# The S5 stage of a two-layer decoder trunk: copies of g as own steps, a new plan of steps, later tables loaded behind a weight

## The chip, the core and the metric

The kernel runs on one core of a Trainium2 chip. A core has several engines that each work through their own list of instructions in order and wait for one another through semaphores: TensorE (PE in the profile; its weight loads are PEld) multiplies matrices into psum, VectorE (DVE), ScalarE (ACT) and GpSimd (POOL) work element by element, and SyncE (SP) issues most of the DMA transfers from a queue of its own. The metric is the time of one execution on the device in microseconds (us). Three executions of the kernel before took 980.18, 980.32 and 984.25 us; the median is 980.32.

## The reference

Two layers over a sequence of 256 tokens of width 1024, all in float32. Each layer adds half a SwiGLU, a mixer, and another half SwiGLU to the residual h. The mixer of layer 0 is S5, a diagonal state-space layer with 64 groups of 16 channels and 64 states; that of layer 1 is an attention. The change lies in the S5 mixer, which the reference writes as follows (shapes cut):

```python
u = hn @ w_in                                   # 256 x 1024, hn = RMSNorm(h)
lam = exp((a_re + i a_im) * dt);  bb = coef * b # tables of each group
st[t] = lam * st[t-1] + bb @ u[t]               # complex states, a scan over the 256 tokens
y = re(c @ st) + d_skip * u
g = gelu(y)
g = g * sigmoid(g @ w_glu)
h = h + g @ w_out
```

## The kernel before, in words

The kernel is one long program in six phases: f00 (first SwiGLU), s5, f01, f10, moba, f11. The order of the instructions on each engine is the order in which the Python code emits them (`manual_schedule`). Products in float32 are made of three faster products: every operand is split into a high part, which the fast matmul takes exactly, and a low part (the rest). So a weight unit is loaded into one of three `raw` buffers (1 MB each), then split by halves: ScalarE writes `whi` (line 86, or line 92 where a gain is folded in) and VectorE writes `wlo` (line 87 or 93). `Stream.pump()` emits the next half's split when a slot is free, and when both halves of a unit are split its `raw` buffer is given to the next unit's load on SP's queue. In `plan` strings a pump is the word `P`.

In the phase f00 small pieces of work are dropped between the matmuls by a time plan (`tables`): they compute the tables of S5 (discretised matrices and powers of lambda) and write them to DRAM (`dA`, `dE`, `dB`). When that is done, the function loads them back for blocks b = 0, 1, 2 (lines 957 to 961): TA (512 KB), TE (260 KB), TB (768 KB), with three buffers of each. Later blocks are loaded from within the steps.

In `s5` the 1024 channels are eight blocks b of 128. Its steps, all written out in order in the string `plan`, are:

- `wC.t:k` (w_in): part k of eight of the product with w_in, for columns from C (0, 256, 512; 512 takes 512 columns) and token half t. Three matmuls (lines 399 to 401). After part 7 ScalarE copies the product from psum to `us` (line 1015) and VectorE transposes it into `U` (line 1016). These products live in the two `pM` psum tiles.
- `tb` (t1): 32 small matmul instructions with table TA (line 1025), into `pA` tiles for b below 4 and `pM` tiles above.
- `rb` (rot): ScalarE clears a column and writes `rh` (lines 1036, 1037); VectorE rotates and scans (lines 1044 to 1049); GpSimd rotates back into `hr` (lines 1051 to 1054). TE is the table.
- `yb` (y_out): 48 matmul instructions with TB on U and hr (line 1068) into a `pR` psum tile; gelu on ScalarE (`yg`, line 1072), a transpose on VectorE (`gs`, line 1074).
- `gb` (g_tr): TensorE transposes gs into a `pR` tile (line 1083). For b of 2 and above ScalarE reads the tile into g's high part (line 1086), VectorE into its low part (line 1087). In every case ScalarE then reads it a third time, into `gf` (line 1088), g in full precision. There are two `pR` tiles, shared by y and g steps.
- `ub:o` (glu): output o of eight of g @ w_glu for block b. Blocks 0 and 1 multiply gf with the raw weight in float32 (line 1106); the others use parts (lines 1108 to 1110).

Behind the plan the code issues, in loops, the last two blocks (b = 6, 7) of `glu` by pairs of outputs, each pair followed by `gate(i)` (sigmoid, times gf, split into parts: lines 1119 to 1124), and then the first two blocks of the product with w_out (`so`) with pumps between. `boundary` ends the phase.

Of the kernel before, what the change touches and what calls it, by code (L numbers as in the profile page):

```python
# [12 lines left out]
AF = mybir.ActivationFunctionType  # L13
# [107 lines left out]
def trunk_kernel(ctx: ExitStack, tc, x, ffn_norm, ffn_w_gate, ffn_w_up, ffn_w_down, mix_norm,  # L121
# [3 lines left out]
    nc = tc.nc  # L125
# [13 lines left out]
    def psR():  # L139
        return pp.tile([128, 512], F32, name="pR", tag="R", bufs=2)  # L140

    def psA(i):
        return pp.tile([128, 512], F32, name=f"pA{i}", tag=f"A{i}", bufs=1)
# [12 lines left out]
    where = {}  # L156
    WHOLE = 2
# [73 lines left out]
    def warm(func):  # L231

        w = sp.tile([128, 1], F32, name="warm", tag="warm", bufs=1)
        nc.scalar.activation(w, ones[:, 0:1], func)
# [33 lines left out]
    if "s5" in phases:  # L268
        rho = cp.tile([128, 32], F32, name="rho")
        tstack, lstack, xstack = ExitStack(), ExitStack(), ExitStack()  # L270
# [8 lines left out]
    st = Stream(nc, units, rp, hp)  # L279
# [20 lines left out]
    XP = [xp]  # L300
# [16 lines left out]
    def home(pool, ph):  # L317

        xa = pool.tile([128, 4224], F32R, name="xa")
        v = xa[:, XO[ph]:XO[ph] + 4096].rearrange("p (i k c) -> p i k c", i=2, c=256)  # L320
        return v[:, 0], v[:, 1]
# [298 lines left out]
    def tables(tp):  # L620

        V, P = nc.vector, nc.gpsimd

        def T(name, *shape):
            return tp.tile([128] + list(shape), F32, name=name)
# [41 lines left out]
        ps = psR()  # L667
# [26 lines left out]
        q, y, y2, e0, e1, den = (T(n, 32) for n in ("q", "y", "y2", "e0", "e1", "den"))  # L694
# [20 lines left out]
        ps = psR()  # L715
# [56 lines left out]
        u2, w2 = T("u2", 2, 32), T("w2", 2, 32)  # L772
# [29 lines left out]
        for i, a in enumerate((ltr, lti)):  # L802
            av = a.rearrange("p (b q) s -> p b q s", b=8)
            for k in range(2):
                P.tensor_copy(L[i][:, :, 0, k], av)
                for s in range(3):
                    o = L[i][:, :, 1, k, :, s]
# [131 lines left out]
        while work or later or dma:  # L939
# [4 lines left out]
            if later and later[0][0] <= now:  # L944
                f = later.pop(0)
                f[1](*f[2:])
                done[0] += 1
            while work and work[0][1] <= now and credit >= work[0][0] and done[0] >= work[0][4]:
                w, _, f, pe, _ = work.pop(0)
                f[0](*f[1:])  # L950
                credit -= w
                t = max([now + LAG] + [a[0] + PACE for a in later])
# [1 line left out]
            yield  # L954
        tstack.close()
        LP.append(lstack.enter_context(tc.tile_pool(name="load", bufs=3)))
        for b in range(3):
            ld_a(b)
            ld_e(b)
        for b in range(3):  # L960
            ld_b(b)

    LP, TA, TE, TB = [], {}, {}, {}

    def ld_a(b):
        TA[b] = LP[0].tile([128, 1024], F32, name="TA", bufs=3)
        nc.sync.dma_start(TA[b], dA[b])

    def ld_e(b):
        TE[b] = LP[0].tile([128, 2, 4, 65], F32, name="TE", bufs=3)  # L970
        nc.sync.dma_start(TE[b], dE[b // 4].rearrange("p (i q c) -> p i q c", i=2, c=65)[:, :, (b % 4) * 4:(b % 4) * 4 + 4])

    def ld_b(b):
        TB[b] = LP[0].tile([128, 1536], F32, name="TB", bufs=3)
        nc.sync.dma_start(TB[b], dB[b])


    def s5(nxt, entry):
        V, P = nc.vector, nc.gpsimd
        HALVES = (slice(0, 64), slice(64, 128))  # L980
        wstack = ExitStack()
        wp = wstack.enter_context(tc.tile_pool(name="s5", bufs=1))
        S, H, W = {}, {}, {}
        GT, GS = {}, {}
        acc = [None] * 4

        U = wp.tile([128, 32, 2, 32], F32, name="U")
        gf = [fp.tile([128, 640], F32, name="gf", tag=("ah", "al")[i // 2], bufs=2)[:, 0:512]
              .rearrange("p (f c) -> p f c", c=256) for i in range(4)]
# [87 lines left out]
        def g_tr(b):  # L1077
            if b == WHOLE:
                GT["h"], GT["l"] = home(xp, "g")
            ps = psR()  # L1080
            gs = GS.pop(b)
            for t in range(2):
                nc.tensor.transpose(ps[:, t * 128:(t + 1) * 128], gs[:, t].rearrange("p q c -> p (q c)"),
                                    ident)
            if b >= WHOLE:
                nc.scalar.activation(GT["h"][:, b, :], ps[:, 0:256], AF.Copy)
                V.tensor_tensor(GT["l"][:, b, :], ps[:, 0:256], GT["h"][:, b, :].bitcast(F32), op=OP.subtract)
            nc.scalar.activation(gf[b // 2][:, b % 2, :], ps[:, 0:256], AF.Copy)

        def glu(b, os):  # L1090

            u = where["glu", b // 2]
            g = gf[b // 2][:, b % 2, :]
            if b < WHOLE:
                w = st.raw[u][:, b % 2 * 1024:b % 2 * 1024 + 1024]
            else:
                gh, gl = GT["h"][:, b, :], GT["l"][:, b, :]
                wh, wl = st.get(u, b % 2)
            for o in os:
                first, last = b == 0 and o % 2 == 0, b == NB - 1  # L1100
                if first:
                    acc[o // 2] = psA(o // 2)
                d = acc[o // 2][:, (o % 2) * 256:(o % 2) * 256 + 256]
                c = slice(o * 128, o * 128 + 128)
                if b < WHOLE:
                    mm(d, w[:, c], g, start=first, stop=last, skip_group_check=True)  # L1106
                else:
                    mm(d, wh[:, c], gh, start=first, stop=False, skip_group_check=True)
                    mm(d, wh[:, c], gl, start=False, stop=False, skip_group_check=True)
                    mm(d, wl[:, c], gh, start=False, stop=last, skip_group_check=True)  # L1110
                if o == 7 and b >= WHOLE:
                    st.release(u, b % 2)
                elif o == 7 and b % 2:
                    st.free_raw(u)

        def gate(i):

            sg = fp.tile([128, 2, 256], F32, name="sg", tag="gr", bufs=2)
            nc.scalar.activation(sg, acc[i].rearrange("p (a c) -> p a c", a=2), AF.Sigmoid)
            g = gf[i]  # L1120
            V.tensor_tensor(g, g, sg, op=OP.mult)
            gh, gl = (GT[p][:, 2 * i:2 * i + 2, :] for p in "hl")
            nc.scalar.activation(gh, g, AF.Copy)
            V.tensor_tensor(gl, g, gh.bitcast(F32), op=OP.subtract)

        def so(b, t, n, last=False):
            u = where["so", b]
            if b == 0:
                acc[2 * t + n] = psA(2 * t + n)
            gh, gl = (GT[p][:, 2 * b:2 * b + 2, :] for p in "hl")  # L1130
            bank_mm(acc, t, n, gh, gl, u, [0, 1], b == 0, last)

        def step(word):
            name, _, ks = word.partition(":")
            ks = [int(k) for k in ks.split("-")] if ks else []
            ks = range(ks[0], ks[-1] + 1) if ks else ()
            if name[0] == "w":
                c0, t = name[1:].split(".")
                for k in ks:
                    w_in(int(c0), int(t), k)  # L1140
            elif name[0] == "u":
                glu(int(name[1]), ks)
            elif name == "x":
                if entry:
                    prep(1, 1, "s5")
            elif name == "P":
                st.pump()
            elif name in ("gelu", "sigmoid"):
                warm(AF.Gelu_apprx_tanh if name == "gelu" else AF.Sigmoid)
            else:  # L1150
                {"t": t1, "r": rot, "y": y_out, "g": g_tr}[name[0]](int(name[1]))

        plan = """
            w0.0:0-1 P x w0.0:2-5 P w0.0:6 w0.1:0 w0.0:7 w0.1:1-4 P w0.1:5-7 w256.0:0-4 w256.1:0-1 t0 w256.0:5
            w256.1:2 P w256.0:6 r0 w256.1:3 w256.0:7 P t1 w512.0:0 w256.1:4-7 w512.0:1 r1 w512.0:2-3 t2 gelu
            r2 t3 y0 w512.0:4-5 w512.1:0-1 w512.0:6 w512.1:2 r3 w512.1:3-4 w512.0:7 w512.1:5 y1 w512.1:6-7 g0
            y2 P P u0:0-1 g1 t4 u0:2-3 r4 g2 u0:4 t5 u0:5-7 r5 u1:0 t6 y3 u1:1-2 r6 u1:3-7 u2:0-2 t7 y4 g3
            u2:3-5 r7 y5 u2:6-7 u3:0-2 y6 g4 u3:3-4 g5 u3:5-7 P u4:0 P u4:1 P u4:2 g6 y7 u4:3-4 P P u4:5-7  # L1160
            u5:0-1 sigmoid g7 u5:2-5 P u5:6-7 P
        """
        for word in plan.split():
            step(word)
        wstack.close()
        lstack.close()
        XP[0] = xstack.enter_context(tc.tile_pool(name="xt2", bufs=1))
        for i in range(4):
            glu(6, (2 * i, 2 * i + 1))
            glu(7, (2 * i, 2 * i + 1))  # L1170
            gate(i)
        for b in range(2):
            for t in range(2):
                for n in range(2):
                    so(b, t, n)
                if t == 1:
                    for i in range(2):
                        st.release(where["so", b], i)
                st.pump(2 - b * t)

        boundary(nxt, [lambda t, n: so(2, t, n), lambda t, n: so(3, t, n, True)], acc, 1.0, pumps=(1, 2))
        for b in (2, 3):
            for i in range(2):
# [157 lines left out]


    tab = tables(tabp) if "s5" in phases else iter(())
    next(tab, None)
    slot = [0]
# [42 lines left out]
    v2, rn, r2 = (sp.tile([128, 2], F32, name=n, tag=n, bufs=1) for n in ("ms2", "rn2", "rr2"))  # L1388
# [29 lines left out]
    ps = psR()  # L1418
# [72 lines left out]
```

## Time and profile before

| what | value |
|---|---|
| median of three executions | 980.32 us |
| the profiled execution | 980.45 us |
| its span, first to last instruction | 978.6 us |
| TensorE busy | 968.7 us, 99% of the span |
| VectorE, ScalarE, GpSimd busy | 690.0, 556.1, 211.8 us |
| granted TensorE clock | 1.000 |
| S5 phase in the profile | about 209.7 to 301.8 us |

How to read the rows: a row of a timeline has the start in us, the duration in us, the engine, the line of the kernel, the operation, the tiles (written <- read), the shapes, the count, and in brackets how long the engine stood idle ahead of it and what it waited for. A row of the waits has who waited and for whom, then the total in us, the number of waits and the longest. A row of the windows has the stretch, its length, and then for TensorE, its weight loads, VectorE, ScalarE and GpSimd the busy time (with the number of instructions), the granted clock, the busy share of the DMA engines and the GB/s. A row of the chain of waits has the start, the duration and the piece of work. A row of the DMA issues has the count, the size and the median us from issue to landing. A matmul's duration covers its way through the array; the next one starts before it ends, so what one costs is the distance between starts. Instructions that repeat within a row are counted after an x.

### The profile page before, as it was taken

The page shows a single profiled execution, that of the slowest core. Times are in us where ns is not written, and L with a number is a line of the kernel's source. Part 1 is how long each engine was busy: PE and PEld are TensorE (multiplying, and loading weights), DVE is VectorE, ACT ScalarE, POOL GpSimd, SP SyncE. Part 2 cuts the span into 40 slices and gives each one's busy share as a digit, 9 for nine tenths or more (in the row PEclk, how much of TensorE's full clock was granted, in tenths as well). Part 3 has the DMA queues.
Part 4 walks back from the last instruction along what each step waited for, and adds up shares of the span by engine and source line. Part 5 has one row for each costly group of instructions (what it writes and reads, how often), then busy time and mean ns, then how long its engine had stood idle before and what let it go on. Part 6 is the DMA issues. An engine that isn't in the chain of part 4 may idle for free.

```text
span 978.6 us, 17165 instructions
## 1 busy us (share of the span) xinstructions
PE 968.7 (99%) x6695; PEld 864.0 (88%) x6695; DVE 690.0 (71%) x1118; ACT 556.1 (57%) x1008; POOL 211.8 (22%) x381
## 2 busy tenths in 40 slices
PE   9999999999999999999999999999999999999998
PEld 7878787888888999999999999998888899999997
DVE  5898878667767776666567766665789667766662
ACT  7655676453377565555456555554897566655550
POOL 5961889516501000000010000000441010000000
PEclk9999999999999999999999999999999999999999
DMA  8999999987646656565546656562544646656531
GB/s 286 263 306 300 286 287 292 270 318 239 228 172 208 214 184 213 173 216 172 172 129 216 218 179 207 173 215 92 173 155 147 199 140 214 222 176 212 172 130 43
DMA packets 145505, 200.92 MB, mean 205 GB/s; under 512 B 20152, under 2 KB 117520, under 8 KB 145168
## 3 DMA queue, kind: packets, MB, share of 16 engines
q1 hardware_dynamic: 138032, 188.51, 59.4%
q0 software_dynamic: 6816, 10.71, 4.1%
q8 instruction: 52, 0.85, 0.4%
q10 hardware_dynamic: 576, 0.61, 0.3%
q14 instruction: 29, 0.24, 0.1%
HBM read 183.89 MB, written 15.76 MB: 204 GB/s over the span
## 4 chain that ended last, share of the span: by engine, by line
PE 88%; DVE 4%; POOL 2%; DMA 2%; ACT 2%; issue 1%; SPq 0%; ACTq 0%; POOLq 0%
PE pM L554 13%; PE pM L553 13%; PE pM L555 13%; PE pA L399 9%; PE pA L401 9%; PE pA L400 9%; PE pM L399 6%; PE pM L400 5%; PE pM L401 5%; DVE wlo L87 2%; DMA raw<-in_s_w_in_dram 1%; PE pR L1068 1%; POOL sc L686 1%; PE pA L1106 1%; PE pR L333 1%
## 5 line engine op out<-in xcount | busy, mean ns | idle before, releaser
L553 PE MATMUL pM<-xa,whi 128*128 128x256 f32 x1056 | 295.7, 280 | 0.0
L554 PE MATMUL pM<-xa,whi 128*128 128x256 f32 x1056 | 294.9, 279 | 0.0
L555 PE MATMUL pM<-xa,wlo 128*128 128x256 f32 x1056 | 294.6, 279 | 0.0
L93 DVE SCALAR_TENSOR_TENSOR wlo<-raw,gT,whi 128x512 fp32r<-128x512 f32 x328 | 228.1, 747 | 72.0 <-ACT whi L92 71.8
L92 ACT ACTIVATE whi<-raw,gT 128x512 fp32r<-128x512 f32 x328 | 213.8, 711 | 19.9 <-PE pA L401 15.5
L87 DVE TENSOR_TENSOR wlo<-raw,whi 128x1024 fp32r<-128x1024 f32 (+1 forms) x155 | 188.5, 1230 | 48.9 <-ACT whi L86 47.7
L554 PEld LDWEIGHTS pM<-xa,whi 128*128 128x128 f32 x1056 | 198.5, 188 | 2.6
L553 PEld LDWEIGHTS pM<-xa,whi 128*128 128x128 f32 x1056 | 198.5, 188 | 2.3
L555 PEld LDWEIGHTS pM<-xa,wlo 128*128 128x128 f32 x1056 | 198.5, 188 | 0.0
L86 ACT ACTIVATE whi<-raw 128x1024 fp32r<-128x1024 f32 (+1 forms) x155 | 159.3, 1050 | 29.5 <-DMA raw<-in_ffn_w_up_dram 11.0
L399 PE MATMUL pA<-whi,ah 128*128 128x512 f32 x352 | 138.6, 394 | 0.0
L401 PE MATMUL pA<-whi,al 128*128 128x512 f32 x352 | 137.6, 391 | 0.0
L400 PE MATMUL pA<-wlo,ah 128*128 128x512 f32 x352 | 137.6, 391 | 0.0
L399 PE MATMUL pM<-whi,xa 128*128 128x512 f32 (+1 forms) x304 | 121.8, 401 | 1.3 <-ACT us L1015 1.3
L568 ACT ACTIVATE sg<-gr 128x256 f32<-128x256 f32 x66 | 27.6, 418 | 165.7 <-DVE gr L565 165.7
L400 PE MATMUL pM<-wlo,xa 128*128 128x512 f32 (+1 forms) x304 | 115.8, 381 | 0.1
L401 PE MATMUL pM<-whi,xa 128*128 128x512 f32 (+1 forms) x304 | 115.4, 380 | 0.0
L348 POOL TENSOR_TENSOR ms<-ss 128x1 f32<-128x1 f32 x10 | 1.9, 194 | 473.2 <-ACT sq L345 473.2
L401 PEld LDWEIGHTS pA<-whi,al 128*128 128x128 f32 x352 | 66.1, 188 | 14.3
L399 PEld LDWEIGHTS pA<-whi,ah 128*128 128x128 f32 x352 | 66.1, 188 | 11.6
L400 PEld LDWEIGHTS pA<-wlo,ah 128*128 128x128 f32 x352 | 66.2, 188 | 11.4
L565 DVE TENSOR_TENSOR gr<-pM,rrow 128x512 f32<-128x512 f32 x66 | 45.5, 689 | 40.8 <-PE pM L555 40.7
(271 smaller groups left out, 1234.4 us busy)
## 6 DMA issues: line engine op xcount, KB each, us to landing
raw<-in_ffn_w_down_dram SPq DMA_DIRECT2D x44, 1024.0 KB, 5.4
raw<-in_ffn_w_gate_dram SPq DMA_DIRECT2D x80, 512.0 KB, 4.1
raw<-in_ffn_w_up_dram SPq DMA_DIRECT2D x80, 512.0 KB, 5.2
raw<-in_moba_w_qkv_dram SPq DMA_DIRECT2D x12, 1024.0 KB, 5.2
TB<-dB SPq DMA_DIRECT2D x8, 768.0 KB, 6.6
raw<-in_ffn_w_gate_dram SPq DMA_DIRECT2D x16, 256.0 KB, 4.3
raw<-in_ffn_w_up_dram SPq DMA_DIRECT2D x16, 256.0 KB, 4.7
dA<-blank SPq DMA_DIRECT2D x8, 512.0 KB, 9.9
```

What stands on the lines that cost most here:

```text
L86: nc.scalar.activation(hi[:, c], r[:, c], AF.Copy)
L87: nc.vector.tensor_tensor(lo[:, c], r[:, c], hi[:, c].bitcast(F32), op=OP.subtract)
L92: nc.scalar.activation(hi[:, c], r[:, c], AF.Identity, scale=g)
L93: nc.vector.scalar_tensor_tensor(lo[:, c], r[:, c], g, hi[:, c].bitcast(F32), op0=OP.mult, op1=OP.subtract)
L399: mm(o, xh, wh, start=start, stop=False)
L400: mm(o, xh, wl, start=False, stop=False)
L401: mm(o, xl, wh, start=False, stop=stop)
L553: mm(o, a, xh, start=k == 0 and i == 0, stop=False, skip_group_check=True)
L554: mm(o, a, xl, start=False, stop=False, skip_group_check=True)
L555: mm(o, b, xh, start=False, stop=k == 7, skip_group_check=True)
L565: V.tensor_tensor(gr, ps.rearrange("p (i c) -> p i c", i=2), Rr["row"][:, None, :].to_broadcast([128, 2, 256]), op=OP.mult)
L568: nc.scalar.activation(sg, gr[:, 0, :], AF.Silu)
```

## The change

Four things change, all in the S5 phase.

1. The third read of the psum tile in `g_tr`, the copy into `gf`, becomes a step of its own, `fb` (function `g_f`). For blocks 0 and 1 it is still emitted at once; for blocks 2 to 7 it stands where the plan says. The psum tile is kept until then (`GP`).
2. `tables` loads back TA and TE of blocks 0 and 1 only. TA and TE of block 2 and TB of blocks 0 to 2 are loaded at the start of `s5`. On SP's queue the fourth unit of w_in and the first unit of w_glu, which followed these loads, now precede them.
3. The loops behind the plan become steps (`a` for a gate, `o` for a part of the w_out product), so that pumps can stand between them.
4. The plan is laid out anew: same steps, another order, `P` in other places.

```diff
@@ tables
         LP.append(lstack.enter_context(tc.tile_pool(name="load", bufs=3)))
-        for b in range(3):
+        for b in range(2):
             ld_a(b)
             ld_e(b)
-        for b in range(3):
-            ld_b(b)
@@ s5, g_tr
             if b >= WHOLE:
                 nc.scalar.activation(GT["h"][:, b, :], ps[:, 0:256], AF.Copy)
                 V.tensor_tensor(GT["l"][:, b, :], ps[:, 0:256], GT["h"][:, b, :].bitcast(F32), op=OP.subtract)
-            nc.scalar.activation(gf[b // 2][:, b % 2, :], ps[:, 0:256], AF.Copy)
+            GP[b] = ps
+            if b < WHOLE:
+                g_f(b)
+
+        def g_f(b):
+            if b in GP:
+                nc.scalar.activation(gf[b // 2][:, b % 2, :], GP.pop(b)[:, 0:256], AF.Copy)
@@ s5, step
+            elif name[0] == "a":
+                if name == "a0":
+                    wstack.close()
+                    lstack.close()
+                    XP[0] = xstack.enter_context(tc.tile_pool(name="xt2", bufs=1))
+                gate(int(name[1]))
+            elif name[0] == "o":
+                b = int(name[1])
+                for k in ks:
+                    so(b, k // 2, k % 2)
+                    if k == 3:
+                        for i in range(2):
+                            st.release(where["so", b], i)
@@ s5, the plan
         plan = """
-            w0.0:0-1 P x w0.0:2-5 P w0.0:6 w0.1:0 w0.0:7 w0.1:1-4 P w0.1:5-7 w256.0:0-4 w256.1:0-1 t0 w256.0:5
-            w256.1:2 P w256.0:6 r0 w256.1:3 w256.0:7 P t1 w512.0:0 w256.1:4-7 w512.0:1 r1 w512.0:2-3 t2 gelu
-            r2 t3 y0 w512.0:4-5 w512.1:0-1 w512.0:6 w512.1:2 r3 w512.1:3-4 w512.0:7 w512.1:5 y1 w512.1:6-7 g0
-            y2 P P u0:0-1 g1 t4 u0:2-3 r4 g2 u0:4 t5 u0:5-7 r5 u1:0 t6 y3 u1:1-2 r6 u1:3-7 u2:0-2 t7 y4 g3
-            u2:3-5 r7 y5 u2:6-7 u3:0-2 y6 g4 u3:3-4 g5 u3:5-7 P u4:0 P u4:1 P u4:2 g6 y7 u4:3-4 P P u4:5-7
-            u5:0-1 sigmoid g7 u5:2-5 P u5:6-7 P
+            w0.0:0-1 P x w0.0:2-5 P w0.0:6-7 w0.1:0-7 w256.0:0-2 w256.1:0 w256.0:3 w256.1:1 P t0 P w256.0:4
+            w256.1:2 r0 w256.1:3 gelu t1 f0 w256.0:5 w256.1:4 w256.0:6 w256.1:5 w256.0:7 r1 w256.1:6-7
+            w512.0:0 P w512.0:1-4 w512.1:0-1 w512.0:5-7 y0 f1 P t2 t3 r2 w512.1:2 g0 w512.1:3-4 u0:0 r3 u0:1
+            w512.1:5 u0:2 w512.1:6-7 u0:3-4 y1 y2 t4 r4 g1 u0:5 g2 u0:6 y3 t5 t6 u0:7 u1:0-4 r5 u1:5-6 r6 f2
+            u1:7 u2:0-3 g3 t7 r7 f3 y4 y5 u2:4-6 P u2:7 u3:0-3 g4 f4 u3:4 P u3:5-6 y6 u3:7 u4:0 g5 u4:1 P P
+            u4:2 y7 P u4:3-5 f5 u4:6-7 u5:0-1 P g6 u5:2-4 sigmoid g7 u5:5 f6 u5:6 P u5:7 f7 u6:0-1 u7:0-1 a0
+            u6:2-3 u7:2-3 a1 u6:4-5 u7:4-5 a2 P u6:6-7 u7:6-7 a3 P P P o0:0-3 o1:0-2 P o1:3 P
         """
+        ld_a(2)
+        ld_e(2)
+        for b in range(3):
+            ld_b(b)
         for word in plan.split():
             step(word)
-        for i in range(4):
-            glu(6, (2 * i, 2 * i + 1))
-            glu(7, (2 * i, 2 * i + 1))
-            gate(i)
-        for b in range(2):
-            for t in range(2):
-                for n in range(2):
-                    so(b, t, n)
-                ...
-                st.pump(2 - b * t)
```

The words f0 and f1 of the plan do nothing, since those copies are emitted in `g_tr`. At the start of the next phase, f01, two halves of its weights fewer have been split than before, and the first product there splits them in its own course.

More of the change, by code (lines that the diff above doesn't have):

```diff
@@ L983, in s5 @@
         S, H, W = {}, {}, {}
-        GT, GS = {}, {}
+        GT, GS, GP = {}, {}, {}
         acc = [None] * 4
@@ L1150, in step @@
             else:
-                {"t": t1, "r": rot, "y": y_out, "g": g_tr}[name[0]](int(name[1]))
+                {"t": t1, "r": rot, "y": y_out, "g": g_tr, "f": g_f}[name[0]](int(name[1]))
         plan = """
-            w0.0:0-1 P x w0.0:2-5 P w0.0:6 w0.1:0 w0.0:7 w0.1:1-4 P w0.1:5-7 w256.0:0-4 w256.1:0-1 t0 w256.0:5
-            w256.1:2 P w256.0:6 r0 w256.1:3 w256.0:7 P t1 w512.0:0 w256.1:4-7 w512.0:1 r1 w512.0:2-3 t2 gelu
-            r2 t3 y0 w512.0:4-5 w512.1:0-1 w512.0:6 w512.1:2 r3 w512.1:3-4 w512.0:7 w512.1:5 y1 w512.1:6-7 g0
-            y2 P P u0:0-1 g1 t4 u0:2-3 r4 g2 u0:4 t5 u0:5-7 r5 u1:0 t6 y3 u1:1-2 r6 u1:3-7 u2:0-2 t7 y4 g3
-            u2:3-5 r7 y5 u2:6-7 u3:0-2 y6 g4 u3:3-4 g5 u3:5-7 P u4:0 P u4:1 P u4:2 g6 y7 u4:3-4 P P u4:5-7
-            u5:0-1 sigmoid g7 u5:2-5 P u5:6-7 P
-        """
+            w0.0:0-1 P x w0.0:2-5 P w0.0:6-7 w0.1:0-7 w256.0:0-2 w256.1:0 w256.0:3 w256.1:1 P t0 P w256.0:4
[5 more added lines that the diff above has]
+            u6:2-3 u7:2-3 a1 u6:4-5 u7:4-5 a2 P u6:6-7 u7:6-7 a3 P P P o0:0-3 o1:0-2 P o1:3 P
+        """
+        ld_a(2)
+        ld_e(2)
+        for b in range(3):
+            ld_b(b)
         for word in plan.split():
             step(word)
-        wstack.close()
-        lstack.close()
-        XP[0] = xstack.enter_context(tc.tile_pool(name="xt2", bufs=1))
-        for i in range(4):
-            glu(6, (2 * i, 2 * i + 1))
-            glu(7, (2 * i, 2 * i + 1))
-            gate(i)
-        for b in range(2):
-            for t in range(2):
-                for n in range(2):
-                    so(b, t, n)
-                if t == 1:
-                    for i in range(2):
-                        st.release(where["so", b], i)
-                st.pump(2 - b * t)
         boundary(nxt, [lambda t, n: so(2, t, n), lambda t, n: so(3, t, n, True)], acc, 1.0, pumps=(1, 2))
```

## The prediction

> **What bounds the kernel now.** I read the page first, then what TensorE waited for, then the stretch of the S5 stage, and last TensorE's own rows in time.
>
> ```profile
> span 978.6 us, 17165 instructions
> PE 968.7 (99%) x6695; PEld 864.0 (88%) x6695; DVE 690.0 (71%) x1118; ACT 556.1 (57%) x1008; POOL 211.8 (22%) x381
> ...
> PE pM L399 <- ACT us L1015: 1.3, 1, 1.3
> PE pR L1083 <- DVE gs L1074: 1.1, 1, 1.1
> ...
> PE pM L1025 <- issue: 0.3, 1, 0.3
> ...
> 209.70:301.80 92.10, 89.26 (x1055) 78.56 (x1053) 69.60 (x109) 46.03 (x90) 34.37 (x47) 1.00 0.67 236
> ```
>
> The first two lines are the page: TensorE is busy for 99% of the span. The next three are its waits in S5 (two more, at lines 1385 and 830, lie before it): 2.7 us. The last line is the S5 stage (92.10 us; TensorE 89.26, VectorE 69.60, ScalarE 46.03, GpSimd 34.37; clock granted 1.00). No other engine fills the stage, so its length is TensorE's issue time plus the places where TensorE stands still. The change removes no matmul; it can only take back standing time. How much there is shows in the starts of matmuls:
>
> ```profile
> 217.18 0.28 PE L401 MATMUL pM<-whi,xa 128*128 128x256 f32 x1
> ...
> 217.54 0.28 PE L401 MATMUL pM<-whi,xa 128*128 128x256 f32 x1
> 219.09 0.38 PE L399 MATMUL pM<-whi,xa 128*128 128x256 f32 x1 [1.28 <-ACT us L1015]
> ...
> 274.69 0.28 PE L1110 MATMUL pA<-xa,wlo 128*128 128x256 f32 x1
> 276.06 0.30 PE L1083 MATMUL pR<-cst,gs 128*128 128x128 f32 x1 [1.09 <-DVE gs L1074]
> ...
> 279.18 0.39 PE L1108 MATMUL pA<-xa,whi 128*128 128x256 f32 x1
> 279.63 0.38 PE L1109 MATMUL pA<-xa,whi 128*128 128x256 f32 x1
> ...
> 284.99 0.40 PE L400 MATMUL pA<-wlo,xa 128*128 128x512 f32 x1
> 285.38 0.50 PE L401 MATMUL pA<-whi,xa 128*128 128x512 f32 x1
> ```
>
> Three matmuls of 256 columns start within 0.36 us (217.18 to 217.54), so one is worth 0.12 us of issue. 217.54 to 219.09 is 1.55 us, of which 1.43 are lost; 274.69 to 276.06 loses 1.25; 279.18 to 279.63 loses 0.33; 284.99 to 285.38 loses 0.16 (a matmul of 512 columns is worth 0.23, see below). With the 0.33 before t6 (the line "L1025 <- issue") S5 holds 1.43 + 1.25 + 0.33 + 0.33 + 0.16 = 3.5 us of standing still. That is the most the change can bring on this path, 0.36% of the time.
>
> **The later loads, behind the gate weight.** The chain of waits (its first row here) and ScalarE's rows in time show what made the first loss:
>
> ```profile
> 204.44 12.88 DMA raw<-in_s_w_in_dram
> ...
> 217.35 1.33 ACT L92 ACTIVATE whi<-raw,gT 128x512 fp32r<-128x512 f32 x2 [2.23 <-DMA raw<-in_s_w_in_dram]
> 218.59 0.45 ACT L1015 ACTIVATE us<-pM,rr 128x256 f32<-128x256 f32 x1
> ```
>
> The last unit of w_in is issued at 204.44, behind nine loads of tables, and lands 12.88 us later; ScalarE stands in front of its split, and the copy `us` of the finished product w0.1 queues behind, so its psum tile is not free for w256.1:0. The change issues TA2, TE2 and TB0 to TB2 after this unit and after the first w_glu unit on SP's queue.
>
> ```profile
> TB<-dB SPq DMA_DIRECT2D x3, 768.0 KB, 9.3
> TA<-dA SPq DMA_DIRECT2D x4, 512.0 KB, 5.2
> raw<-in_s_w_in_dram SPq DMA_DIRECT2D x1, 1024.0 KB, 12.9
> TE<-dE SPq DMA_DIRECT2D x3, 260.0 KB, 6.3
> GB/s 113 30 25 0 0 63 296 372 210 265 225 315 298 343 330 400 413 412 444 425 416 444 378 454 416 384 381 394 350 400 394 406 403 416 410 397 416 290 164 44
> ```
>
> These are the transfers between 196 and 222 us. 512 + 260 + 3 x 768 KB = 3.1 MB no longer lie ahead of the w_in unit; at the 400 GB/s of that stretch this is 7.7 us, so it lands near 209.6 instead of 217.3. Its split moves to behind w256.1:1, some 218, so it is 8 us early. In return 2.1 MB go ahead of the TB loads: 5.2 us. TB0, at 202.24 + 9.3 us before, comes near 217, TA2 near 213; y0 and t2 read them at some 231 and 232 (below). Cost nothing: 14 us of w_in matmuls cover it. Even at half the rate (ten us later) y0 has them.
> And `us` of w0.1 is now ahead of the split on ScalarE: w256.0:0-2 (three parts of three matmuls, 1.08 us) lie between w0.1:7 and w256.1:0, and the copy needs 0.28 (the last matmul's length) + 0.45 (its own) with two passes between engines at 0.05 (us ends at 219.04, the matmul that it frees starts at 219.09): 0.83. In time by 0.25. The 1.43 are gone.
>
> **g's copy as a step of its own.**
>
> ```profile
> 270.92 3.50 DVE L87 TENSOR_TENSOR wlo<-raw,whi 128x1024 fp32r<-128x1024 f32 x3 [1.40 <-ACT whi L86]
> ...
> 274.78 0.38 ACT L1088 ACTIVATE gf<-pR 128x256 f32<-128x256 f32 x1 [1.73 <-DVE xa L1087]
> 275.06 0.38 ACT L1072 ACTIVATE yg<-pR 128x256 f32<-128x256 f32 x1
> ```
>
> g_tr reads its psum tile three times: `xa` on ScalarE (L1086), `xa` on VectorE (L1087), `gf` on ScalarE (L1088); the third waits for the second. Here VectorE does three splits of weights (3.50 us) first, so ScalarE stands for 1.73 us at gf, and the gelu of y7 (L1072) starts at 275.06 only. Its transpose gs then lets g7 go at 276.06: the 1.25. In the new plan g5's copy f5 comes behind y7 and two splits, so the gelu of y7 waits for y7 and for ScalarE's own splits only. Adding the steps up (below) y7 starts at 267.7 and ends at 269.4; two splits of 1.17 stand ahead of gs on VectorE, until 271.3, and gs ends at 271.7; g7 stands at 273.1. In time by 1.3.
> The price is a psum tile held longer: pR has two, and y or g two steps later waits for f. By the same adding up g1's is freed at 246.5 for y3 at 246.9, g3's by f3 at 258.5 for y5 at 258.9, g5's at 271.1 for g6 at 271.8. Margins 0.3 to 0.7, so nothing as long as ScalarE is no later than this.
>
> **The plan laid out anew.** All steps are the same; prices come from these rows.
>
> ```profile
> 220.07 1.08 PE pA L1025 x32
> ...
> 230.57 1.40 PE pR L1068 x48
> ...
> 253.89 3.22 PE pA L1106 x14
> ...
> 227.94 0.39 PE L400 MATMUL pM<-wlo,xa 128*128 128x512 f32 x1
> 228.17 0.39 PE L401 MATMUL pM<-whi,xa 128*128 128x512 f32 x1
> 228.49 0.33 PE L1025 MATMUL pA<-U,TA 128*64 128x63 f32 x4
> ...
> 231.18 0.67 DVE L1044 TENSOR_TENSOR wv<-pA,TE 128x512 f32<-128x512 f32 x1
> ...
> 233.52 1.26 DVE L1049 TENSOR_TENSOR_SCAN zo<-rh,pA 128x256 f32<-128x256 f32 x2
> ...
> 231.40 1.19 POOL L1051 TENSOR_TENSOR pv<-zo,TE 128x512 f32<-128x512 f32 x1 [1.45 <-issue]
> ...
> 234.51 0.74 POOL L1054 TENSOR_TENSOR hr<-pv,pv 128x256 f32<-128x256 f32 x1
> ```
>
> t costs 1.08, y 1.40, a column of u0/u1 0.46 (3.22 by seven), a w512 part 3 x 0.23 = 0.69, a rotation 231.18 to 234.78 = 3.6 on VectorE and 231.40 to 235.25 = 3.85 on GpSimd. From w512 to t the start-to-start is 0.32, 0.09 above 0.23; back I take the same, so an excursion into plain f32 work costs some 0.2. By the plans there are 11 before and 14 after (the g steps standing alone counted), but 3 of the added ones are lone g's, which in before cost the same inside a longer run, and changes between u0/u1 and t or y fall from 7 to 4 at some 0.1. I take 0, between -0.3 and +0.6.
> Adding the steps up from 217.54 (the 21st part of 256 columns): part 22 ends 217.9, t0 is done at 219.1, ten parts and t1 bring w512.0:0 to 224.0, ten w512 parts bring y0 to 231, t2 and t3 end at 234.6, the rest of w512.1 with g0 and u0:0-4 brings y1 to 241.7, y2 to 243.1, y3 to 246.9, t6 to 249.6. Against that:
> - us of w256.0 has only w256.1:6-7 (0.72) to finish in 0.83 before w512.0:0: 0.1 late.
> - r0 ends on VectorE at 223.6 (behind two halves of weights), on GpSimd at 227.5; y0 at 231 is safe. r2 follows t2: VectorE 235.2 to 238.8, GpSimd to 242.6, 0.5 ahead of y2; r3 to 246.5, 0.4 ahead of y3.
> - t6 takes the pM tile that r4's scan frees at some 249.5: 0 to 0.3 late, as before (the 0.33).
> - u6:0 reads g6's low part, behind two splits on VectorE: 0 to 0.4 late (was u7's 0.33). The gates then find VectorE free, and o0 no longer waits (the 0.16).
> New waits: 0.1 + 0.1 + 0.3 = 0.5, between 0 when all passes are quick and 1.3 when each is 0.1 slower.
>
> **The next stage.** At its start two halves fewer are split ahead.
>
> ```profile
> 311.82 3.78 ACT L92 ACTIVATE whi<-raw,gT 128x512 fp32r<-128x512 f32 x6
> ...
> 312.57 4.07 DVE L93 SCALAR_TENSOR_TENSOR wlo<-raw,gT,whi 128x512 fp32r<-128x512 f32 x6 [0.53 <-ACT whi L92]
> ```
>
> The first pair of this run becomes the fourth half of f01's first product, needed (on the clock of before) at 313.3 by ScalarE's part and 313.5 by VectorE's; they are there at 312.5 and 313.3. I price it at 0, with 0.3 as the other end.
>
> **Sum.** -3.5 + 0.5 + 0 + 0 = -3.0 us. The profiled execution took 980.45 us (span 978.6 and 1.85 around it), 0.13 above the median of 980.32, so 977.45 for it and 977.3 for the median. Ends: 980.32 - 3.5 - 0.3 = 976.5; and 980.32 - 3.5 + 1.3 + 0.6 + 0.3 = 979.0. What a measurement can tell here is about 0.5%, 4.9 us; the forecast is inside it.
>
> **Rivals.**
> *VectorE and GpSimd block each other.* Here is how a split fares beside GpSimd:
>
> ```profile
> 225.29 2.10 DVE L87 TENSOR_TENSOR wlo<-raw,whi 128x1024 fp32r<-128x1024 f32 x1
> ...
> 226.26 2.19 POOL L1052 TENSOR_TENSOR pv<-zo,TE 128x512 f32<-128x512 f32 x1
> ```
>
> A split alone takes 1.17 (3.50 by three) and a pv 1.19; meeting, 2.10 and 2.19. Two splits of the new plan fall into rotations (behind w512.0:0 with r1, behind u2:6 with r7). If two more meet, each adds 0.9 to 1.0 on VectorE ahead of low parts, gs and the psum tiles freed by f, whose margins are 0.3 to 0.7: 0.4 each, 0.8 for two at least, 1.8 if they also hold r2 and r3. 978.1 to 979.6. For it: r2 to r7 run closer on GpSimd; against it: both sure meetings lie where margins are over 3 us or 0.5. The Trainium skill (SBUF — State Buffer, Who interferes with whom) says that a VectorE instruction with two SBUF inputs and a GpSimd one that reads SBUF take a shared pair of ports in turn, the loser blocked for the whole instruction; by that rule, the trace agrees: 2.10 is 0.93 of standing and its own 1.17. By a share of bandwidth instead, later meetings would cost less and this rival would shrink to nothing.
> *The tile held by f (slower than before).* If ScalarE reaches f1, f3, f4 and f5 late, because the low parts before them on VectorE queue behind splits (1.73 us in the row above), y3, y5, g5 and g6 each wait some 1.73 - 0.5 = 1.2 us: 4 x 1.2 = 4.9 against 3.0 gained, 982.2. It decides from 0.75 us of mean wait at these four on. Against it: only f4 and f5 have splits just ahead.
> *No change.* If t6, u6 and the copy at w512.0:0 take all that the two large waits give back, 980 to 980.5. Their rows of before show 0.33 at most each, so this needs them to grow fourfold.
>
> **How the numbers follow.** Forecast 0.71, its own range 976.5 to 979.0; ports 0.14; held tile 0.07; no change 0.05; more gain than counted (the next stages start earlier and lose a wait of their own) 0.03. Down to 976.0 and up to 980.6 leaves out the held tile and most of the last. A gain above 4.9 us has no standing time to come from in S5: 0.02. A loss above 4.9 needs the held tile at more than twice its price: 0.04. The rest, 0.94, lies within.
>
> **What would show it.** Right: no wait at us of w0.1 and none at gs of y7 in TensorE's waits; w_in's last unit landing within 10 us; t0 starting at 218, and the second matmul of o0 (284.99 before) near 281.9. Wrong: waits of y3, y5, g5 or g6 on gf; of y2, y3 on hr; of f01's first product on whi or wlo; or a split beside pv above 2 us more than twice.

## The result, and the profile after

Six executions of the changed kernel took 974.58 to 975.62 us, median 974.97; six of the kernel before have the median 980.6. The ratio is 0.9936, with a 95% interval of 0.9924 to 0.9948: faster by 5.6 us between the medians, just over the 0.5% that a measurement can tell, and 2.6 us more than forecast. The profiled execution took 974.58 us (span 972.8; before 978.6).

The page, TensorE's waits over the whole span, and the S5 stage among the windows, of the kernel after:

```profile
span 972.8 us, 17168 instructions
PE 965.9 (99%) x6695; PEld 863.7 (89%) x6695; DVE 690.1 (71%) x1118; ACT 555.7 (57%) x1008; POOL 211.6 (22%) x381
...
PE pR L1392 <- POOL ones L229: 1.0, 1, 1.0
PE pR L830 <- DVE al L500: 0.8, 1, 0.8
...
209.50:296.00 86.50, 86.49 (x1055) 78.47 (x1054) 67.56 (x104) 43.73 (x86) 35.20 (x47) 1.00 0.71 253
```

The two waits left lie outside S5; inside it the view shows none. The stage is 86.5 us long where it was 92.1, and TensorE is busy for 86.49 of it. S5 begins 0.2 us earlier than before, and from its end to the end of the program the distance to before stays at 5.83 to 5.85 us. So the gain, but for those 0.2, is made in S5, and the stage after it takes nothing back.

TensorE's rows at the places where it stood, and the other rows that the prediction leaned on (ScalarE's split of the late weight, the transfers from 196 to 222 us, VectorE and GpSimd meeting):

```profile
217.59 0.28 PE L400 MATMUL pM<-wlo,xa 128*128 128x256 f32 x1
217.71 0.28 PE L401 MATMUL pM<-whi,xa 128*128 128x256 f32 x1
217.91 0.86 PE L1023 MATMUL pA<-U,TA 128*64 128x63 f32 x22
...
272.65 0.28 PE L1114 MATMUL pA<-xa,wlo 128*128 128x256 f32 x1
272.77 0.38 PE L1081 MATMUL pR<-cst,gs 128*128 128x128 f32 x2
...
279.67 0.40 PE L399 MATMUL pA<-whi,xa 128*128 128x512 f32 x1
279.91 0.40 PE L400 MATMUL pA<-wlo,xa 128*128 128x512 f32 x1
...
216.42 2.55 ACT L92 ACTIVATE whi<-raw,gT 128x512 fp32r<-128x512 f32 x4
...
raw<-in_s_w_in_dram SPq DMA_DIRECT2D x1, 1024.0 KB, 8.1
...
228.12 2.15 DVE L87 TENSOR_TENSOR wlo<-raw,whi 128x1024 fp32r<-128x1024 f32 x1
...
229.15 2.17 POOL L1050 TENSOR_TENSOR pv<-zo,TE 128x512 f32<-128x512 f32 x1
```

t0 starts at 217.91; g7 starts at 272.77, 0.12 behind its forerunner, without a wait; the second matmul with w_out follows the first by 0.24, and the forecast 281.9 for it became 279.91. The weight lands in 8.1 us instead of 12.9, and ScalarE takes its split without standing.

To see the rest I set every start of a matmul in S5 against the plain distances of its kind: 0.117 us for 256 columns of split numbers, 0.227 for 512, 0.211 for a row of u0/u1, 0.034 for t, 0.029 for y. What goes beyond these sums to:

| in S5, us beyond the plain distances | before | after | change |
|---|---|---|---|
| five waits over 0.25 us | 3.69 | 0 | -3.69 |
| short stands: first w_out products, the matmuls just behind a wait, and what is left | 1.43 | 0.59 | -0.84 |
| going into and out of runs of t and y | 4.91 | 3.19 | -1.72 |
| inside those runs (below zero: the 0.034 for t is too large, its matmuls start about 0.030 apart) | -1.71 | -1.26 | +0.45 |
| around g steps, and between f32 and split numbers | 0.68 | 0.87 | +0.19 |
| sum | 8.99 | 3.38 | -5.61 |

The third row is what the prediction had not seen. The t and y steps use matmuls on 64 columns of the array (`128*64` in the rows); everything else uses 128. Unbroken runs of t and y: 12 before, 8 after, 4.91 / 12 = 0.41 and 3.19 / 8 = 0.40 us each. That is theory 1: each run on 64 columns costs TensorE about 0.4 us at its two ends (less what comes back inside it, the row below), and the new order has four runs fewer. Theory 2 is the prediction's: what costs is the change between plain f32 and split numbers. The experiments first take the change apart, then set these two against each other. The stage S5 starts between 209.3 and 210.3 us in all runs, and the difference is there already at 65 us, in stages that no edit touches; so lengths of the stage are compared.

### The profile page after: what moved, and what is told of

The parts are those of the page before. It is cut to its first block, busy times and chain, and to the rows that moved or that the text cites. A ratio compares the mean times of both kernels' runs of the same rounds, so it can differ in the third digit from the quotient of the medians.

```text
span 972.8 us, 17168 instructions
## 1 busy us (share of the span) xinstructions
PE 965.9 (99%) x6695; PEld 863.7 (89%) x6695; DVE 690.1 (71%) x1118; ACT 555.7 (57%) x1008; POOL 211.6 (22%) x381
## 4 chain that ended last, share of the span: by engine, by line
PE 94%; DVE 3%; POOL 2%; issue 0%; ACT 0%; ACTq 0%; POOLq 0%
PE pM L554 13%; PE pM L553 13%; PE pM L555 13%; PE pA L399 9%; PE pA L401 9%; PE pA L400 9%; PE pM L399 6%; PE pM L400 6%; PE pM L401 6%; PE pR L1066 1%; DVE wlo L87 1%; PE pR L333 1%; POOL sc L686 1%; PE pA L1110 1%; PE pA L1112 1%; PE pA L473 1%
```

## Experiments: the parts of the change

**Loads alone, on the kernel before.**

```diff
         # tables
-        for b in range(3): ld_a(b); ld_e(b)
-        for b in range(3): ld_b(b)
+        for b in range(2): ld_a(b); ld_e(b)
         # s5, ahead of the old plan
+        ld_a(2); ld_e(2)
+        for b in range(3): ld_b(b)
```

> Before with one part of the change alone: the loads of TA2, TE2 and the three TB are issued behind the first units of W_in; f copies and order of steps are those of before. If the 1.43 us in front of w256.1:0 is the late landing of W_in's last unit, that wait goes or shrinks to the split's own end: stage S5 shorter by 1.2 to 1.5 us (92.1 to about 90.7), everything else of the stage as it was. If the landing is hidden anyway by the split ahead of it in ScalarE's queue: 92.1 as before, the wait stays at 1.4.

978.98 us, ratio 0.9978 (0.9965 to 0.9990). The stage is 90.97 us, 1.12 shorter. TensorE's waits in it:

```profile
PE pR L1081 <- DVE gs L1072: 1.1, 1, 1.1
PE pR L333 <- DVE h L371: 0.4, 1, 0.4
PE pM L1023 <- issue: 0.3, 1, 0.3
```

The wait at `us` of 1.3 is gone from the list (1.44 by distance), so the late weight was its cause. 0.34 of it comes back at the boundary, where VectorE's `h` (line 371) is now what the next transposes wait for: 0.60 by distance, 0.26 before.

**Loads put back, in the kernel after.**

```diff
         # tables
-        for b in range(2): ld_a(b); ld_e(b)
+        for b in range(3): ld_a(b); ld_e(b)
+        for b in range(3): ld_b(b)
         # s5, ahead of the new plan
-        ld_a(2); ld_e(2)
-        for b in range(3): ld_b(b)
```

> After with the loads of the later tables put back at the head of the stage; new order of steps and copies as steps kept. If the new order alone hides the landing of W_in's last unit (w256.1:0 stands later in it): S5 within 0.2 us of 86.5. If the loads' place is worth by itself what the prediction gave it: a wait of 1 to 1.4 us in front of the first matmul of w256.1 or of w0.1, S5 about 87.7.

975.21 us, ratio 0.9938 (0.9916 to 0.9960); S5 86.64 against 86.48, and no wait. ScalarE's rows show why:

```profile
216.16 0.48 ACT L1015 ACTIVATE us<-pM,rr 128x256 f32<-128x256 f32 x1 [1.11 <-POOL rr L310]
217.27 2.56 ACT L92 ACTIVATE whi<-raw,gT 128x512 fp32r<-128x512 f32 x4 [0.63 <-DMA raw<-in_s_w_in_dram]
```

The weight again lands at 217.25 and ScalarE stands 0.63 for it, but the copy `us` is already ahead of the split, and the split is not yet needed. So in the new order the loads' new place is worth nothing that can be told from noise: order and loads each remove the same 1.4.

**The copy f6 alone, on the kernel before.**

```diff
         # g_tr: only block 6 keeps its psum tile
+            GP[b] = ps
+            if b != 6: g_f(b)
         # plan
-            ... g6 y7 u4:3-4 ...
+            ... g6 y7 f6 u4:3-4 ...
```

> Before with one other part alone: only the copy of g6 into the second table becomes a step of its own, behind y7. If the wait of 1.25 us at g7 is that copy standing ahead of the copy of y7 on ScalarE: g7 comes 0.6 to 0.9 us earlier, the stage is 91.2 to 91.5. If VectorE's splits ahead of the subtraction for gs7 are what comes last: no more than 0.2 us.

979.75 us, ratio 0.9986 (0.9972 to 1.0001); S5 92.02, 0.07 shorter. The waits:

```profile
PE pM L399 <- ACT us L1015: 1.3, 1, 1.3
PE pA L1113 <- ACT xa L1086: 0.5, 1, 0.5
PE pM L1025 <- issue: 0.3, 1, 0.3
PE pR L1083 <- DVE gs L1074: 0.2, 1, 0.2
PE pR L333 <- DVE h L371: 0.2, 1, 0.2
```

By distance the stand ahead of g7 fell from 1.26 to 0.37, as forecast by the first reading. But a new one of 0.66 stands 3.75 us later (line 1113, waiting for g7's high part on ScalarE), and the boundary loses 0.07 more. The gain came where it was expected and was given back one step on: with the old order ScalarE is short of time at this place, and one copy's place only chooses who waits.

**All copies at once again, in the kernel after.**

```diff
             GP[b] = ps
-            if b < WHOLE:
-                g_f(b)
+            g_f(b)
```

> After with every copy of g made at once in g's own step, as before, order of steps and loads as after. If the copies' place is what keeps the waits away: new waits at u4, g5, y7, g7, u6 and u7 of together 3 to 5 us, S5 89.5 to 91.5. If the copies are hidden wherever they stand and the order of TensorE's matmuls alone makes the gain: S5 within 0.5 us of 86.5.

980.14 us, ratio 0.9994 (0.9981 to 1.0008); S5 91.98, 5.50 longer than after. The waits, then two windows of this kernel (granted clock third from last):

```profile
PE pA L1111 <- ACT xa L1084: 1.3, 1, 1.3
PE pA L1112 <- DVE xa L1085: 1.0, 1, 1.0
PE pR L1081 <- DVE gs L1072: 0.2, 1, 0.2
...
276.40:279.80 3.40, 1.56 (x8) 1.16 (x9) 0.80 (x3) 2.49 (x6) 0.00 (x0) 1.00 1.00 400
279.80:283.20 3.40, 3.40 (x18) 3.40 (x17) 1.83 (x2) 2.02 (x4) 0.00 (x0) 0.50 0.31 125
```

The waits over 0.25 us come to 3.3 us by distance, all behind 274 us (g7, u6, u7), where 3 to 5 were expected and more places named. Another 1.5 us nobody expected: behind the last two stands the granted clock falls to 0.50 for 3.4 us, and sixteen matmuls of 256 columns start 0.213 apart instead of 0.117. The remaining 0.6 or so lies in shorter stands and was not followed up. The clock is not what decides, though: two of the ten executions of this kernel were granted 1.000 throughout and still took 979.35 and 980.13 us, where the six granted 0.998 have a mean of 980.18. Neither was profiled, so where they spent the time is open. So the copies as steps of their own are what lets the new order keep its gain; without them it is no faster than before.

## Experiments: what a run of t and y costs

**Runs broken up by f32 columns of 128.**

```diff
-            ... u0:3-4 y1 y2 t4 r4 g1 u0:5 g2 u0:6 y3 t5 t6 u0:7 u1:0-4 ...
+            ... u0:3 y1 u0:4 y2 u0:5 t4 r4 g1 u0:6 g2 y3 u0:7 t5 u1:0 t6 u1:1-4 ...
```

> After with the runs of matmuls on 64 columns of the array (t and y) broken up by columns of u0 and u1 (plain f32, 128 columns) between them: 12 runs of t and y as in before, instead of 8; same matmuls, same copies. Theory 1, each run of t and y between matmuls of 128 columns costs about 0.4 us (0.16 in, 0.23 out): S5 longer by 1.4 to 1.8 us, no new waits. Theory 2, the cost is that of changing between plain f32 and split numbers (the prediction's term): u0, u1, t and y are all plain f32, so S5 stays within 0.3 us.

976.3 us, ratio 0.9948 (0.9935 to 0.9960); S5 87.59, 1.11 longer than after, no new wait. y1 and y2, each with its column of u0, in this kernel:

```profile
240.90 0.34 PE L1066 MATMUL pR<-U,TB 128*64 128x64 f32 x4
...
242.45 0.70 PE L1110 MATMUL pA<-gf,raw 128*128 128x256 f32 x2
243.08 0.34 PE L1066 MATMUL pR<-U,TB 128*64 128x64 f32 x4
```

From 240.90 to 243.08 is 2.18 us; 48 y matmuls at 0.029 and two of u0 at 0.211 are 1.82. Going out and in costs 0.36, though u0 and y are both plain f32. Theory 2 had said at most 0.3 for the whole and falls; theory 1 had the sign and the place, but 1.4 to 1.8. At the ends of the runs the four added ones do cost 1.64; 0.45 comes back inside the runs, t6's wait of 0.13 and the changes from one step to the next (0.07 from y1 to y2) among it. Net, a run costs 1.11 / 4 = 0.28 us here: the 0.4 read from the ends alone is too high.

**f32 columns strewn among split ones.**

```diff
-            ... u1:0-4 r5 u1:5-6 r6 f2 u1:7 u2:0-3 g3 ...
+            ... u1:0-3 r5 r6 f2 u2:0 u1:4 u2:1 u1:5 u2:2 u1:6 u2:3 u1:7 g3 ...
```

> After with the last four columns of u1 (plain f32, 128 columns) put singly between columns of u2 (split numbers, 128 columns): four more runs of plain f32. Theory 1 (width of the array in use): S5 within 0.3 us. Theory 2 (plain f32 against split numbers, 0.2 a run): S5 longer by about 0.8 us.

975.42 us, ratio 0.9939 (0.9925 to 0.9952); S5 86.66, 0.17 longer, and by distance most of it lies elsewhere: the changes between f32 and split numbers sum to 0.10 where they summed to 0.05.

```profile
252.31 0.47 PE L1112 MATMUL pA<-xa,whi 128*128 128x256 f32 x1
252.61 0.28 PE L1113 MATMUL pA<-xa,whi 128*128 128x256 f32 x1
252.72 0.28 PE L1114 MATMUL pA<-xa,wlo 128*128 128x256 f32 x1
252.84 0.60 PE L1110 MATMUL pA<-gf,raw 128*128 128x256 f32 x2
253.08 0.47 PE L1112 MATMUL pA<-xa,whi 128*128 128x256 f32 x1
```

One round of three split matmuls and two f32 ones takes 253.08 - 252.31 = 0.77; 3 x 0.117 + 2 x 0.211 is 0.77. The first start looks early and the second late (0.30), and the two cancel: a reader who looks at one distance only would price this change at 0.19.

**The cost by itself.** A block of matmuls on constants stands behind the last one of the program; it alternates stretches of two kinds, four times each.

```diff
+    def wide(n, m, z):                    # 128 columns, n moving
+        for _ in range(m):
+            mm(px[:, 0:n], z[:, 0:128], z[:, 0:n], start=True, stop=True)
+    def half(n, m):                       # both halves of 64 columns
+        for _ in range(m):
+            for r in HALVES:
+                mm(px[r, 0:n], xf[:, r], xf[:, 0:n], start=True, stop=True)
+    # stretches: half(64, 24) with wide(256, 4, xf); half(256, 4) with wide(256, 4, xf);
+    # wide(64, 24, xf) with wide(256, 4, xf); half(64, 24) with wide(64, 24, xf);
+    # wide(256, 8, xr) with wide(256, 4, xf); half(64, 24) with wide(256, 8, xr)
```

> After with a block of matmuls added behind the last one of the program, on constants and read by nobody; the output stays as it is, the added time is not the question. Stretches of four kinds alternate four times each: f32 on 64-column halves with 64 moving columns (as t and y), the same with 256 moving columns, f32 on 128 columns with 64 and with 256 moving columns, and split numbers on 128 columns with 256. Theory 1, the width of the array in use is what costs: about 0.35 to 0.45 us beyond the plain pitches for each going to 64-column halves and back, with 64 or 256 moving columns, against f32 and against split numbers alike; under 0.1 us between 128-column matmuls of 64 and 256 moving columns, and between f32 and split ones. Rival A, the short moving operand costs: 128 columns with 64 moving columns show the 0.4 too, 64-column halves with 256 moving columns do not. Rival B, the kind of number: only the f32 and split pair shows it.

TensorE's rows (an f32 matmul makes two records; xf is f32, xr is in the fast form of the split parts):

```profile
978.86 3.02 PE L1471 MATMUL pA<-xf 128*64 128x64 f32 x96
981.81 1.99 PE L1466 MATMUL pA<-xf 128*128 128x256 f32 x8
983.73 3.02 PE L1471 MATMUL pA<-xf 128*64 128x64 f32 x96
...
998.35 1.95 PE L1471 MATMUL pA<-xf 128*64 128x256 f32 x16
...
1002.15 1.95 PE L1471 MATMUL pA<-xf 128*64 128x256 f32 x16
...
1011.63 30.34 PE L1466 MATMUL pA<-xf 128*128 128x256 f32 x232
1041.90 3.02 PE L1471 MATMUL pA<-xf 128*64 128x64 f32 x96
...
1050.35 3.02 PE L1471 MATMUL pA<-xf 128*64 128x64 f32 x96
...
1076.62 1.89 PE L1466 MATMUL pA<-xf 128*128 128x256 f32 x8
...
1079.30 1.89 PE L1466 MATMUL pA<-xf 128*128 128x256 f32 x8
...
1086.48 3.02 PE L1471 MATMUL pA<-xf 128*64 128x64 f32 x96
...
1090.57 3.02 PE L1471 MATMUL pA<-xf 128*64 128x64 f32 x96
```

Within a stretch the records start 0.216 apart (128 columns, 256 moving), 0.112 (128 columns, 64 moving), 0.119 (split form), and a pair of halves 0.216 or, with 64 moving, 0.0585. What one there-and-back takes beyond these:

| alternation | from start to start | plain | beyond |
|---|---|---|---|
| halves, 64 moving / 128 f32 | 983.73 - 978.86 = 4.87 | 48 x 0.0585 + 8 x 0.216 = 4.53 | 0.34 |
| halves, 256 moving / 128 f32 | 1002.15 - 998.35 = 3.80 | 16 x 0.216 = 3.45 | 0.35 |
| halves / 128 f32, 64 moving | 1050.35 - 1041.90 = 8.45 | 48 x 0.0585 + 48 x 0.112 = 8.18 | 0.27 |
| halves / 128 split | 1090.57 - 1086.48 = 4.09 | 48 x 0.0585 + 8 x 0.119 = 3.76 | 0.33 |
| 128 f32 / 128 split | 1079.30 - 1076.62 = 2.68 | 8 x 0.216 + 8 x 0.119 = 2.68 | 0.00 |

And the long row at 1011.63, in which 128-column matmuls of 64 and 256 moving columns alternate unbroken by halves, takes 30.27 up to the next row, 192 x 0.112 + 40 x 0.216 = 30.14 by the plain distances, so nothing for eight changes beyond the 0.1 at either end. Rival A (the short moving operand) and rival B (the kind of number) fall; the width of the array in use is what costs, 0.27 to 0.35.

The weight loads show the form of this price. Here is TensorE going into y6, in the kernel after:

```profile
263.67 0.28 PE L1113 MATMUL pA<-xa,whi 128*128 128x256 f32 x1
263.68 0.19 PEld L1114 LDWEIGHTS pA<-xa,wlo 128*128 128x128 f32 x1
263.79 0.28 PE L1114 MATMUL pA<-xa,wlo 128*128 128x256 f32 x1
264.00 0.20 PEld L1066 LDWEIGHTS pR<-U,TB 128*64 128x64 f32 x4
264.00 0.34 PE L1066 MATMUL pR<-U,TB 128*64 128x64 f32 x4
```

The weights for line 1114 are loaded while the matmul ahead of it has just begun. The first weights of the new width are loaded only 0.07 us before the last matmul of the old width ends (263.79 + 0.28 = 264.07; such ends are modelled by the profile). So it is at all sixteen changes of width in S5 of the kernel after, into 64 columns and out, and at those of the block; between matmuls of one width that follow without a wait, the load is at least 0.13 ahead of that end. The Trainium skill (TensorEngine Tiling (Array Packing), Key Properties) says that changing the tiling mode, as against changing the tile within a mode, drains TensorE; it gives no price. The trace agrees, by these late weight loads, and puts the price of the way there and back at 0.27 to 0.35 us here.

**Fewer runs still.** Two kernels try to go on from 8: one puts t0 beside t1 and y6 beside y7, the other only t0 beside t1.

```diff
-            ... P t0 P w256.0:4 w256.1:2 r0 w256.1:3 gelu t1 f0 ...
+            ... P P w256.0:4 w256.1:2 w256.1:3 gelu t0 t1 r0 f0 ...
     # and, in the first of the two only
-            ... u3:5-6 y6 u3:7 u4:0 g5 u4:1 P P u4:2 y7 P u4:3-5 f5 u4:6-7 ...
+            ... u3:5-7 u4:0 g5 u4:1 f5 P P u4:2 y6 y7 P u4:3-7 ...
```

> After with t0 beside t1 and y6 beside y7, so that there are 6 runs of t and y instead of 8; f5 stands earlier for it. Theory 1 (0.4 us a run): S5 shorter by 0.6 to 0.8 us where no new wait comes (the copies of y6 and y7 follow each other on ScalarE, which may cost 0.2 to 0.4 at g6 or g7). Theory 2: both places lie between split numbers, so two excursions of 0.2 go too: 0.4 us shorter.

> After with t0 beside t1 and nothing else moved (y6, y7 and f5 stay): 7 runs of t and y instead of 8. Theory 1 (0.4 us a run): S5 shorter by 0.3 to 0.4 us, 0.0004 of the run. Rival: t0 comes a microsecond later, and so the rotation of part 0 and its first reader y0 (which had no wait in after); then a wait at y0 of up to 1 us in its place.

With both, 977.55 us, ratio 0.9957 (0.9944 to 0.9971), S5 89.68: 3.20 longer than after, not 0.6 shorter. The ends of the runs fell as theory 1 has it (2.42 us for six), but the waits came back:

```profile
PE pA L1113 <- DVE xa L1085: 1.9, 2, 1.0
PE pR L1066 <- ACT gf L1092: 0.7, 2, 0.4
...
253.93 0.69 DVE L1042 TENSOR_TENSOR wv<-pM,TE 128x512 f32<-128x512 f32 x1 [1.09 <-DMA TE<-dE]
```

By distance they are 3.3 us at four places. Two of them, 1.65 us, are those of the edit alone: y7 waits 0.59 for the psum tile that f5 reads, at 269.08, and behind the two close copies a column of u waits 1.06 for a low part of g, at 276.94. Before the other two, y5 at 258.34 (0.49) and a column of u4 at 265.71 (1.14), a rotation on VectorE stood 1.09 for its table TE (the row at 253.93), ahead of everything that this kernel does otherwise than the one with t0 and t1 alone. The wait at y5 follows from it, as far as the rows show. That at u4 does so only in part: in the kernel with t0 and t1 alone, g4's low part is done at 265.19 and its reader in u4 starts at 266.18, behind y6, which with its two ends takes about 1.75 there. Without y6 ahead of it the reader would come at about 264.4 and wait some 0.8 even with the table as it was there (an estimate from these times). So about 2.4 of the 3.3 us are the edit's. The table TE was issued at 245.46 and took 8.4 us here; in the kernel with t0 and t1 alone it took 7.8 and VectorE stood 0.24, and in after 7.1 with no stand. Why the same transfer was slower is open. With t0 beside t1 alone it is 974.64 us, ratio 0.9941 (0.9927 to 0.9954), S5 86.32: 0.16 shorter, no wait, and y0 in time. The ends gave 0.4 and the w256 part took 0.2 more; the run cannot be told from the kernel after.

## Why the prediction was wrong

It foresaw the direction and, for the two large waits, the reasons, and missed the size: 5.6 us instead of 3.0, outside its range of 976.0 to 980.6.

*The later loads, and `us`: right in time, half right in cause.* t0 was forecast for 218 and came at 217.91, w512.0:0 for 224.0 and came at 223.92; the weight was to land near 209.6 and landed at 209.30. The wait is gone. But the run with the loads put back shows that the new order alone takes it away too.

*g's copy as a step: right.* g7 has no wait, nor have y3, y5, g5 and g6 on f, and taking the copies back costs 3.3 us of waits. f6 alone, however, would have been worth 0.07, not 1.25: the prediction priced the stand at g7 as the copy's and did not ask what f6 itself would be late for in the old order.

*The rivals.* One split met GpSimd (2.15 beside 2.17 us) and another was stretched to 1.82; neither cost TensorE anything. The held tile did not come in after, and did come in the kernel with y6 beside y7 (0.7 us by its list of waits): the mechanism exists, and the margins of the kernel after are wide enough for it. The next stage was priced at 0 and was 0.

*Where the sum failed.* Three terms:
- "an excursion into plain f32 work costs some 0.2 ... I take 0, between -0.3 and +0.6". This is the step that failed. It sorted the changes by kind of number and so counted 11 before and 14 after. The rows that it quoted (228.17 to 228.49) showed the entry into a run of `128*64`, 0.09, and the price belongs to that width: 12 runs before and 8 after, 0.4 each at the ends, about 0.3 net. Measured: -1.7 at the ends, +0.45 within the runs (t6 among it), +0.2 at g and between numbers, -1.1 together.
- The standing time, "That is the most the change can bring on this path", 3.5 us. By distance it was 5.1, and 4.5 of it went. What the 3.5 left out: 0.26 at the boundary, some 0.4 more among the first w_out products than the one 0.16, about 0.2 at the matmuls just behind a wait, and t6's 0.40 instead of 0.33.
- New waits, +0.5: only t6's 0.13 came, and it is counted with the runs above.

-4.5 - 1.1 is the -5.6 found, against -3.5 + 0 + 0.5. That the forecast time of t0 came true says little for the loads, since the new order would have brought it there without them. Which part of the new plan took away the smaller stands (t6, u7, the first w_out products, the boundary) was argued from the order only: no run moves the pumps or the steps behind the old plan by themselves.

## What to carry to other kernels

Order itself has a price on TensorE that no list of waits shows: set the starts of matmuls against their plain distances, sort what is left over by the shape of the array on both sides, and count the unbroken runs of each width before and after a reordering. Keep steps that use part of the array's columns together where their readers allow it, and check with the waits that the merged steps do not ask for the same tiles and the same queue at once. When a stand is put down to one instruction in a queue, ask what is late next once it has gone: of two parts of this change each removed its wait alone, one of them kept 1.1 us of it and the other 0.07.

## What the runs showed of the hardware

Going from 128-column matmuls to 64-column ones and back costs TensorE 0.27 to 0.35 us, whatever the kind of number and the moving length, and going between f32 and split matmuls of 128 columns costs nothing (0.00). At a change of width the first weight load waits until 0.07 us before the end of the last matmul. The second surprise was the clock: two stands of 0.97 and 1.34 us within 3.2 us were followed by 3.4 us at a granted clock of 0.50, worth 1.5 us there, while the stands of 1.28 and 1.09 us in the kernel before, 57 us apart, left it at 1.00. The Trainium skill (TensorE: Matmul & The Clock Gate, What's actually happening) has the clock gate look at TensorE's activity in free-running windows of 3413 ns and halve the clock after an idle one. The length of the stretch at half clock, 3.4 us, agrees with one such window; that it followed one which was not wholly idle (TensorE was busy for 1.56 of the 3.40 us ahead of it) is this one profiled run's and was not tried further.
